# Gates, token projections and pooling input of a two-layer encoder moved to seven block products, with only their seven right operands kept

## Chip, cores and metric

The kernel runs on one core of a Trainium2 chip. The metric is the device time of one execution in microseconds (us); less is better. Engines are named as in the profile: PE is TensorE (matmul), DVE is VectorE, ACT is ScalarE, POOL is GpSimd, SP is SyncE, which issues the loads.

## What is computed

Two layers act on 512 positions of width 1024, all in float32. Cut to what matters:

```
for i in range(2):
    x = LN(a*x + 0.5*swiglu(x, ffn1_up[i], ffn1_down[i]))          # 1024 -> 2*2816 -> 1024
    u,v, q,k,vr,g, pool_in, cq,ckv,kr, gate_logits = split(x @ w_in[i])
    ys = (sgu(u,v), retention(q,k,vr,g), pooling(pool_in), mla(cq,ckv,kr))   # each 256 wide
    merged = sum(sigmoid(gate_logits[:, n]) * (ys[n] @ w_branch[i][n]) for n in range(4))
    x = LN(a*x + merged @ w_out[i])
    ple = sigmoid(x @ w_ple_gate[i]) * (p[i] @ w_ple[i])
    x = LN(a*x + 0.5*swiglu(x, ffn2_up[i], ffn2_down[i]) + ple)
```

w_in has 6304 columns: 512 for sgu (uv), 512 for q and k (qk), 512 for the retention's v and g (vg), 256 for pooling (wp), 416 for latent attention (wm) and 4096 gate columns. The products of x with ffn_up, w_in and w_ple_gate are the "products with the layer's activations" that this document is about.

## The kernel before, in words

**Precision.** Every float32 operand of a large product is kept as a rounded high part and a remainder. `split` (L175) makes them: ACT copies the high part (L177, `whi<-stage`), DVE subtracts it from the source (L178, `wlo<-stage,whi`). `mm3` (L161) then issues three matmuls for each block: low by high, high by low, high by high (L163 to L165).

**Weights.** A weight block of 128x1024 comes by one DMA of 512 KB into a `stage` buffer and is split into a slot, a pair `whi`, `wlo`. There are six slots in a ring and four stage buffers, eight in the feed-forward parts.

**Activations.** After each layer norm the rows are transposed by PE (`lnT`), four 128x128 blocks at a time, and split into `xh`, `xl` (8 x 512 columns). With an index for the half of the features and one for the half of the positions, x consists of B11, B12 (features 0 to 511, positions 0 to 255 and 256 to 511), B21 and B22.

**Seven products.** The feed-forward up-products alone (42 times a unit of 512 output features) are made with seven block products in place of eight (Strassen-Winograd). `up_blocks` (L135) makes the seven left operands from the four weight blocks with four sums on DVE (L138) and seven splits. `unit` (L271) multiplies them with B11, B21, B22 and four combinations T1 to T4 of the B's, kept in `th`, `tl`; each block product is 24 matmuls of 128x256, so 168 a unit. Banks sX, sY and sZ collect them, and three additions on DVE (L289) finish the four result blocks.

**All others are full products.** A gate (`branch`, four branches of eight f's) takes eight weight blocks, 24 matmuls of 128x512, for each f; ACT applies a tanh, six matmuls of 128x512 (`br`) make the branch's output, DVE multiplies and adds. The token projections (`tok_proj`, L580) split four weight blocks and take 24 matmuls of 128x512 for each of the four position blocks: uv, qk, vg, wm (128x416, `mlap`) and the two halves of w_ple_gate (`pg`). The pooling input takes two weight blocks, 24 matmuls each. In layer 1 the first two f's of the first feed-forward part are a full product too (`up`).

**Combinations at the norm.** `norm` (L397) builds T1 to T4 behind the positions 2 and 3 of a norm that precedes a feed-forward part (L428 to L436), not at the norm between the first feed-forward part and the mixers.

**Order.** PE's order is written out by hand: the program text is PE's order, and chains (`norm`, the mixers' small steps) are generators which a weaver (`Weave`) steps when its own clock says that they are ready, or when `need` asks for them. The other engines run their instructions in the order in which the scheduler puts them, each engine in order. In the mixers the order of the program is: uv, sgu, pooling, qk, vg, retention, branch 2, latent attention (`mla`), branches 0, 1, 3, then `w_out` and the norm.

Of the kernel before, what the change touches and what calls it, by code (L numbers as in the profile page):

```python
# [18 lines left out]
P = 128  # L19
# [60 lines left out]
class Trunk:  # L80
# [13 lines left out]

    def __init__(self, tc, ctx, t):
# [8 lines left out]
        self.xh = c.tile([P, KD, SEQ], F32R, tag="xh", name="xh")  # L104
        self.xl = c.tile([P, KD, SEQ], F32R, tag="xl", name="xl")
# [3 lines left out]
        self.tt, self.turn, self.wide = None, False, False  # L109
# [6 lines left out]
    def slot(self):  # L116
        return [self.ring.tile([P, 1024], F32R, tag=q, name=q, bufs=6) for q in ("whi", "wlo")]

    def stage(self):
        self.turn = not self.turn  # L120
        if self.wide and self.turn:
            return self.more.tile([P, 1024], F32, tag="stage", name="stage", bufs=4)
        return self.ring.tile([P, 1024], F32, tag="stage", name="stage", bufs=4)
# [10 lines left out]

    def up_blocks(self, src):  # L135


        add = lambda o, x, y: self.nc.vector.tensor_tensor(o, x, y, op=ALU.add)  # L138

        def get(q):  # L140
            s = self.stage()
            self.load(s, src[:, q, :])
            return s

        a11 = get(0)
        yield self.halves(a11, 1024)
        a21, a22 = get(2), get(3)
        s1 = self.stage()
        add(s1, a21, a22)
        yield self.halves(s1, 1024)  # L150
        add(s1, s1, a11)
        yield self.halves(s1, 1024)
        a12 = get(1)
        yield self.halves(a12, 1024)
        add(a11, a11, a21)
        yield self.halves(a11, 1024)
        add(a12, a12, s1)
        yield self.halves(a12, 1024)
        yield self.halves(a22, 1024)
# [30 lines left out]
    def begin(self, up, fp):  # L190
# [5 lines left out]
        warm = fp.tile([P, SEQ], F32, tag="cc", name="warm", bufs=2)  # L196
        self.nc.vector.memset(warm, 0.0)
        warm = warm.bitcast(F32R)
# [8 lines left out]
        for kk in range(KD // 2):  # L207
# [9 lines left out]
            for j in range(2):  # L217
                self.nc.sync.dma_start(out=x[:, j, :], in_=self.t["xT"][:, 2 * kk + j, :])
                self.split(self.xh[:, 2 * kk + j, :], self.xl[:, 2 * kk + j, :], x[:, j, :])
            for q in range(1, 4):  # L220
                weight(q)
        for kk in range(KD // 2):
            for q, p in enumerate(ps):
                for k in (2 * kk, 2 * kk + 1):
                    self.mm3(p, part([w[0] for w in ws], q, k), part([w[1] for w in ws], q, k),
                             self.xh[:, k, :], self.xl[:, k, :], k == 0, k == KD - 1)
        for j in range(0, HK, 2):
# [4 lines left out]
            for c in range(4):  # L232
                self.split(self.th[:, c, j:j + 2, :], self.tl[:, c, j:j + 2, :], t[c])
# [14 lines left out]
    def open_tt(self):  # L248
        self.tt = ExitStack()
        p = self.tt.enter_context(self.tc.tile_pool(name="tt", bufs=1, reuse_waits="tile"))  # L250
        self.more = p
        self.th, self.tl = [p.tile([P, 4, HK, HT], F32R, tag=q, name=q) for q in ("th", "tl")]

    def close_tt(self):
        self.wide = False
        self.tt.close()

    def open_rows(self):
        self.rows = ExitStack()
        p = self.rows.enter_context(self.tc.tile_pool(name="rows", bufs=1, side="right", reuse_waits="tile"))  # L260
        self.z = [p.tile([P, D], F32, tag=f"z{i}", name=f"z{i}") for i in range(NT)]

    def xop(self, c):

        if c[0] == "T":
            q = int(c[1]) - 1
            return [(self.th[:, q, k, :], self.tl[:, q, k, :]) for k in range(HK)]
        r, s = int(c[1]) - 1, int(c[2]) - 1
        return [tuple(x[:, r * HK + k, s * HT:(s + 1) * HT] for x in (self.xh, self.xl)) for k in range(HK)]

    def unit(self, src, tp):  # L271
# [4 lines left out]
        X, Y, Z = [self.bank(q) for q in ("sX", "sY", "sZ")]  # L276
        cc = tp.tile([P, 2, SEQ], F32, tag="cc", name="cc", bufs=2)
        nb = tp.tile([P, SEQ], F32, tag="nb", name="nb", bufs=2)
        ws = self.up_blocks(src)

        def product(ps, b, first):
            w, x = next(ws), self.xop(b)
            for j in range(2):
                for k, (rh, rl) in enumerate(x):
                    c = slice(j * 512 + k * P, j * 512 + (k + 1) * P)
                    self.mm3(ps[:, j * HT:(j + 1) * HT], w[0][:, c], w[1][:, c], rh, rl,
                             first and j == 0 and k == 0, k == HK - 1, skip_group_check=True)

        add = lambda o, ps: nc.vector.tensor_tensor(o, ps, o, op=ALU.add)  # L289
        product(X, "B11", True)  # L290
        nc.scalar.copy(cc[:, 0], X)
        product(Y, "T1", True)
        nc.scalar.copy(nb, Y)
        product(X, "T2", False)
        nc.scalar.copy(cc[:, 1], X)
        product(Z, "B21", True)
        add(cc[:, 0], Z)
# [99 lines left out]
    def norm(self, z, i, g, b, last, blocks, keep):  # L397
# [15 lines left out]
        for j in range(2):  # L413
# [7 lines left out]
            if not blocks or i < NT // 2:  # L421
                continue
# [679 lines left out]
```

## Time and profile before

| what | value |
|---|---|
| time, median of 3 runs | 2373.01 us (2372.81 to 2373.32) |
| profiled execution, its own time | 2373.37 us |
| its span, first to last instruction | 2371.6 us, so 1.8 us lie around it |
| mean granted TensorE clock | 0.994 of full speed |
| PE busy | 2341.6 us, 99% of the span, 14020 matmuls |
| PE weight loads busy (beside PE) | 2065.3 us, 87% |
| DVE busy | 1572.1 us, 66%, 2230 instructions |
| ACT busy | 908.7 us, 38%, 1200 instructions |
| loads | 246.13 MB, mean 104 GB/s |

The table's shares are means over the whole span. A stage whose engines are loaded in another way is read in the view by windows, which gives each engine's busy time in a stretch. The view of the timeline gives start and duration of single instructions; matmuls overlap, so that the distance of two starts and not the duration tells what one costs.

### The profile page before, as it was taken

What the parts mean: (1) busy time and instruction counts of PE and PEld (TensorE: products, weight loads), DVE (VectorE), ACT (ScalarE), POOL (GpSimd) and SP (SyncE); (2) the same over time, 40 slices, a digit from 0 to 9 for tenths busy, and PEclk for the clock granted to TensorE, in tenths of its full rate; (3) what the DMA queues carried; (4) which work ended last, traced back from release to release, by engine and by line L of the source; (5) the groups of instructions that cost most, each with busy time, mean ns of one, the idle gap of its engine ahead of it and who ended that gap; (6) DMA issues with size and microseconds to landing.
All of it is one profiled execution on the core that took longest, in us unless ns stands there. A gap on an engine that the chain in (4) does not pass through costs nothing.

```text
span 2371.6 us, 33791 instructions
## 1 busy us (share of the span) xinstructions
PE 2341.6 (99%) x14020; PEld 2065.3 (87%) x14020; DVE 1572.1 (66%) x2230; ACT 908.7 (38%) x1200; POOL 55.3 (2%) x93
## 2 busy tenths in 40 slices
PE   9999999999999899999999999999999998999998
PEld 8899897888888698998998998878888886989987
DVE  8777588545445775775896775884454457867757
ACT  6344343234222453443353443442332314534432
POOL 0000001000000000000000000010000000000000
PEclk9999999999999999999999999999999999999999
DMA  6342323222322332423242333232223214323331
GB/s 204 127 125 81 124 98 116 86 82 87 133 98 89 107 106 81 125 82 123 63 135 88 119 104 108 98 122 78 90 80 134 92 60 133 116 80 118 105 107 45
DMA packets 73802, 246.13 MB, mean 104 GB/s; under 512 B 10033, under 2 KB 13233, under 8 KB 73649
## 3 DMA queue, kind: packets, MB, share of 16 engines
q1 hardware_dynamic: 73648, 243.97, 31.9%
q8 instruction: 110, 1.80, 0.3%
q14 instruction: 44, 0.35, 0.0%
HBM read 237.65 MB, written 6.29 MB: 103 GB/s over the span
## 4 chain that ended last, share of the span: by engine, by line
PE 95%; DVE 3%; issue 1%; ACT 1%; DMA 0%; SPq 0%; DVEq 0%; ACTq 0%
PE dn L164 7%; PE dn L165 7%; PE dn L163 7%; PE sX L163 6%; PE sX L165 6%; PE sX L164 6%; PE gate L165 5%; PE gate L163 5%; PE gate L164 5%; PE sY L163 3%; PE sY L165 3%; PE sY L164 3%; PE sZ L164 2%; PE sZ L165 2%; PE sZ L163 2%; PE pg L163 1%
## 5 line engine op out<-in xcount | busy, mean ns | idle before, releaser
L178 DVE TENSOR_TENSOR wlo<-stage,whi 128x1024 fp32r<-128x1024 f32 (+2 forms) x562 | 667.5, 1192 | 431.5 <-ACT whi L177 430.9
L177 ACT CAST whi<-stage 128x1024 fp32r<-128x1024 f32 (+2 forms) x562 | 573.1, 1026 | 615.3 <-PE dn L165 315.8
L163 PE MATMUL sX<-tl,whi 128*128 128x256 f32 x1008 | 282.4, 280 | 0.4 <-DVE nb L289 0.4
L164 PE MATMUL sX<-th,wlo 128*128 128x256 f32 x1008 | 281.4, 279 | 0.4 <-DVE wlo L178 0.3
L165 PE MATMUL sX<-th,whi 128*128 128x256 f32 x1008 | 281.4, 279 | 0.0
L164 PE MATMUL dn<-whi,hp 128*128 128x512 f32 x704 | 278.1, 395 | 1.8 <-DVE hp L178 1.6
L163 PE MATMUL dn<-wlo,hp 128*128 128x512 f32 x704 | 278.8, 396 | 0.0
L165 PE MATMUL dn<-whi,hp 128*128 128x512 f32 x704 | 277.7, 394 | 0.0
L138 DVE TENSOR_TENSOR stage<-stage 128x1024 f32<-128x1024 f32 x168 | 204.7, 1219 | 13.4 <-DMA stage<-up_in 11.9
L163 PE MATMUL gate<-xl,whi 128*128 128x512 f32 x512 | 206.1, 403 | 0.0
L165 PE MATMUL gate<-xh,whi 128*128 128x512 f32 x512 | 202.7, 396 | 0.0
L164 PE MATMUL gate<-xh,wlo 128*128 128x512 f32 x512 | 202.6, 396 | 0.0
L164 PEld LDWEIGHTS sX<-th,wlo 128*128 128x128 f32 x1008 | 189.0, 188 | 0.9 <-DVE wlo L178 0.9
L163 PEld LDWEIGHTS sX<-tl,whi 128*128 128x128 f32 x1008 | 189.2, 188 | 0.6 <-issue 0.6
L165 PEld LDWEIGHTS sX<-th,whi 128*128 128x128 f32 x1008 | 189.5, 188 | 0.0
L164 PEld LDWEIGHTS dn<-whi,hp 128*128 128x128 f32 x704 | 131.9, 187 | 34.3 <-DVE hp L178 3.5
L165 PEld LDWEIGHTS dn<-whi,hp 128*128 128x128 f32 x704 | 131.9, 187 | 32.4
L163 PEld LDWEIGHTS dn<-wlo,hp 128*128 128x128 f32 x704 | 131.9, 187 | 31.1
L632 ACT ACTIVATE gate<-gate 128x512 f32<-128x512 f32 x64 | 38.2, 597 | 228.6 <-PE gate L165 206.3
L165 PEld LDWEIGHTS gate<-xh,whi 128*128 128x128 f32 x512 | 96.3, 188 | 23.0
L164 PEld LDWEIGHTS gate<-xh,wlo 128*128 128x128 f32 x512 | 96.3, 188 | 21.3
L163 PEld LDWEIGHTS gate<-xl,whi 128*128 128x128 f32 x512 | 96.4, 188 | 21.0
(301 smaller groups left out, 4780.6 us busy)
## 6 DMA issues: line engine op xcount, KB each, us to landing
stage<-up_in SPq DMA_DIRECT2D x172, 512.0 KB, 3.9
stage<-dn_in SPq DMA_DIRECT2D x88, 512.0 KB, 3.6
stage<-wg_in SPq DMA_DIRECT2D x64, 512.0 KB, 3.8
stage<-wbr_in SPq DMA_DIRECT2D x16, 512.0 KB, 3.8
stage<-wo_in SPq DMA_DIRECT2D x16, 512.0 KB, 3.6
stage<-wpg_in SPq DMA_DIRECT2D x16, 512.0 KB, 4.0
stage<-wuv_in SPq DMA_DIRECT2D x8, 512.0 KB, 3.5
xs<-z SPq DMA_DIRECT2D x8, 512.0 KB, 2.6
```

The lines of the kernel that those rows point to most:

```text
L138: add = lambda o, x, y: self.nc.vector.tensor_tensor(o, x, y, op=ALU.add)
L163: mm(ps, lh, rl, start=start, stop=False, **more)
L164: mm(ps, ll, rh, start=False, stop=False, **more)
L165: mm(ps, lh, rh, start=False, stop=stop, **more)
L177: self.nc.scalar.copy(hi, src)
L178: self.nc.vector.tensor_tensor(lo, src, hi.bitcast(F32), op=ALU.subtract)
L632: nc.scalar.activation(tg, ps, AF.Tanh, scale=0.5)
```

## The change

1. **One kind of operand.** `xh`, `xl`, `th`, `tl` go; `qh`, `ql` hold seven right operands: B11, B21, B22, T1, T2, T3, T4. B12 is not kept.
2. **All products with the activations are units** (`unit`, L259; `blocks`, L229): a gate unit makes four f's (two units a branch), `tok_unit` (L310) makes uv, qk, vg, the two halves of w_ple_gate and, with 832 columns, wm; wp is a unit of 256 features; the full `up` product in layer 1 becomes a unit. The order of the seven products is B11, B21, then T2, T1, T3, B22, T4.
3. **Early steps.** A unit stops after B11 and B21. Where it is early, this part is issued beside the norm's chain, and weight blocks 0 and 1 are loaded a second time for the sums: uv, qk and vg of each layer, the two halves of w_ple_gate, and the first three up-units of layer 1's first feed-forward part.
4. **Combinations at every norm** but the last, also at that between the first feed-forward part and the mixers.
5. **Space.** Slots: four in the ring, three more in the feed-forward parts only. The rows z stay resident; during the mixers they hold the sums over branches, and the rows come back from scratch behind branch 3. The raw results of the projections are kept in SBUF, and the mixers read them there. Retention's transposes move into its attend chain; the four head chains of `mla` start behind its whole unit, positions 2, 3, 0, 1; branch 2 is followed by a `need` for sgu and retention.

The core of the diff:

```diff
     def slot(self):
-        return [self.ring.tile([P, 1024], F32R, tag=q, name=q, bufs=6) for q in ("whi", "wlo")]
+        self.nslot += 1
+        p, n = (self.more, 3) if self.more and self.nslot % 7 > 3 else (self.ring, 4)
+        return [p.tile([P, 1024], F32R, tag=q, name=q, bufs=n) for q in ("whi", "wlo")]
...
+    def blocks(self, src, n):
...
+        early = (yield) or self.more is None
+        a11 = get(0)
+        yield self.halves(a11, n)
+        a12 = get(1)
+        yield self.halves(a12, n)
+        if early:
+            a11 = get(0)
+        a21, a22 = get(2), get(3)
+        s1 = self.stage()
+        add(s1, a21, a22)
+        add(a21, a21, a11)
+        add(a11, s1, a11)
+        yield self.halves(a11, n)
+        yield self.halves(s1, n)
+        yield self.halves(a21, n)
+        if early:
+            a12 = get(1)
+        add(a12, a12, a11)
+        yield self.halves(a12, n)
+        yield self.halves(a22, n)
...
+        X, Z = bank("sX"), bank("sZ")
+        self.ready(*(range(NT // 2) if not tok else ()))
+        product(X, "B11", True, ws.send(early))
+        nc.scalar.copy(c11, both(X))
+        product(Z, "B21", True, next(ws))
+        v.tensor_tensor(c11, both(Z), c11, op=ALU.add)
+        yield
+        self.ready(*range(NT))
+        Y = bank("sY")
+        product(X, "T2", False, next(ws))
+        nc.scalar.copy(c12, both(X))
+        product(Y, "T1", True, next(ws))
+        nc.scalar.copy(c22, both(Y))
+        product(X, "T3", False, next(ws))
+        v.scalar_tensor_tensor(c22, both(X), -1.0, c22, op0=ALU.mult, op1=ALU.subtract)
+        product(Y, "B22", False, next(ws))
+        v.tensor_tensor(c12, both(Y), c12, op=ALU.add)
+        product(X, "T4", False, next(ws))
+        yield both(X)
...
+            if i < NT // 2:
+                put(j, ps)
+            elif j == 0:
                 self.w.need(self.ln[i - NT // 2])
                 t = self.sums(HK)
...
+            else:
+                put(2, ps)
+                self.combine(t, t[2], part(self.qh, 1).bitcast(F32), ps)
+                nc.vector.tensor_tensor(t[3], t[3], part(self.ql, 1).bitcast(F32), op=ALU.subtract)
+                for c in (1, 2, 3):
+                    put(3 + c, t[c])
...
+            def branch(b, y, first=False, final=None):
+                v = nc.vector
+                for q in range(2):
+                    wb = self.weights(t["wbr"][l, b, q])
...
+                    u = self.unit(t["wg"][l, b, q], 1024, False, G[:, 0:2, a], G[:, 0:2, c], G[:, 2:4, c])
+                    next(u)
...
+                raw = {}
+                for q in ("uv", "qk", "vg"):
+                    raw[q] = cp.tile([P, NT, 512], F32, tag="big8", name=q, bufs=3)
+                us = {q: self.tok_unit(t["w" + q][l], 1024, raw[q], True) for q in raw}
+                for u in us.values():
+                    next(u)
                 y0, y2, y1 = pair(0), pair(2), pair(1)
-                c0 = self.sgu(l, cp, y0)
+                next(us["uv"])
+                c0 = self.sgu(l, cp, y0, raw["uv"])
                 c2 = self.pooling(l, cp, y2)
-                c1 = self.retention(l, cp, y1)
+                next(us["qk"])
+                next(us["vg"])
+                c1 = self.retention(l, cp, y1, raw["qk"], raw["vg"])
                 need(*c2)
-                branch(2, y2)
+                branch(2, y2, True)
                 need(c0)
+                need(c1[0])
+                need(*c1[1])
```

**Where instructions move: DVE, the end of layer 0's norm between the first feed-forward part and the mixers.** z_90 (before) and z_74 (after) are the rows of position block 3. Before:

```order
L406 SCALAR_TENSOR_TENSOR z_90<-z_90,rsln,gb 128x512 x2
L178 TENSOR_TENSOR xl<-lnT,xh 128x4x128
L178 TENSOR_TENSOR wlo<-stage,whi 128x1024 x2
L178 TENSOR_TENSOR xl<-lnT,xh 128x4x128 x2
L923 TENSOR_SCALAR ssq<-ssq 128x512
L924 TENSOR_TENSOR ssq<-ssq,sxh 128x512
```

After:

```order
L420 SCALAR_TENSOR_TENSOR z_74<-z_74,rsln,gb 128x512 x2
L445 TENSOR_TENSOR stage<-ql,lnT 128x512
L446 TENSOR_TENSOR stage<-stage,qh 128x512
L154 TENSOR_TENSOR wlo<-stage,whi 128x1024
L154 TENSOR_TENSOR ql<-stage,qh 128x4x128
L154 TENSOR_TENSOR ql<-lnT,qh 128x4x128
L225 TENSOR_TENSOR stage<-lnT,stage 128x512
L226 SCALAR_TENSOR_TENSOR stage<-stage,lnT 128x512
L295 TENSOR_TENSOR uv<-sZ,uv 128x2x256
L227 SCALAR_TENSOR_TENSOR stage<-stage,qh 128x512
L154 TENSOR_TENSOR ql<-stage,qh 128x4x128
L451 TENSOR_TENSOR stage<-stage,ql 128x512
```

The combinations (L445, L446, L225 to L227, L451, and the splits into ql) now stand between the last norm and the weight splits of the projections, a second such group follows, and the first row of sgu's chain (ssq) stands some 25 rows further on.

**DVE, branch 2 of layer 0, where the gate's weights are split beside the retention's steps.** Before, the first f's:

```order
L859 BN_AGGR gmv<-gst 128x2
L639 SCALAR_TENSOR_TENSOR acc_4255<-gate,br 128x512
L859 BN_AGGR gmv<-gst 128x2
L178 TENSOR_TENSOR wlo<-stage,whi 128x1024
L186 TENSOR_SCALAR rsgn<-gmv 128x4
L861 TENSOR_TENSOR yt<-ro,gmv 128x256
```

After, the first half-branch:

```order
L154 TENSOR_TENSOR wlo<-stage,whi 128x1024 x3
L231 TENSOR_TENSOR stage<-stage 128x1024
L884 TENSOR_TENSOR ke<-qk,dk 128x256
L231 TENSOR_TENSOR stage<-stage 128x1024 x2
L891 TENSOR_TENSOR sd<-rs,dec 128x512
L909 COPY state_4571<-rkv 64x64 x4
L295 TENSOR_TENSOR gate<-sZ,gate 128x2x256
L154 TENSOR_TENSOR wlo<-stage,whi 128x1024 x3
```

One weight split for each f has become a train of seven splits and four sums for four f's, with the additions of the unit (L295) among them.

## Rows read from the trace of the kernel before

**Rows 1.** The page: busy shares, DVE's busy tenths in 40 slices, the load queue.

```profile
PE 2341.6 (99%) x14020; PEld 2065.3 (87%) x14020; DVE 1572.1 (66%) x2230; ACT 908.7 (38%) x1200; POOL 55.3 (2%) x93
...
DVE  8777588545445775775896775884454457867757
...
q1 hardware_dynamic: 73648, 243.97, 31.9%
```

**Rows 2.** The chain that ended last, share of the span by engine.

```profile
PE 95%; DVE 3%; issue 1%; ACT 1%; DMA 0%; SPq 0%; DVEq 0%; ACTq 0%
```

**Rows 3.** Timeline of PE: start and duration in us, then line, operation, tile, shape.

```profile
103.79 0.28 PE L163 MATMUL sX<-xl,whi 128*128 128x256 f32 x1
...
163.21 0.39 PE L163 MATMUL dn<-wlo,hp 128*128 128x512 f32 x1
...
196.81 0.28 PE L163 MATMUL sX<-xl,whi 128*128 128x256 f32 x1
...
507.04 0.35 PE L163 MATMUL mlap<-wlo,xh 128*128 128x416 f32 x1
...
511.92 0.35 PE L165 MATMUL mlap<-whi,xh 128*128 128x416 f32 x1
```

**Rows 4.** DVE's groups by line and shape: busy us, mean ns, idle before.

```profile
L178 DVE TENSOR_TENSOR wlo<-stage,whi 128x1024 fp32r<-128x1024 f32 x534 | 650.2, 1220 | 421.0 <-ACT whi L177 420.3
L138 DVE TENSOR_TENSOR stage<-stage 128x1024 f32<-128x1024 f32 x168 | 204.7, 1219 | 13.4 <-DMA stage<-up_in 11.9
L289 DVE TENSOR_TENSOR cc<-sZ,cc 128x512 f32<-128x512 f32 x42 | 28.8, 685 | 0.7
L178 DVE TENSOR_TENSOR tl<-stage,th 128x512 fp32r<-128x512 f32 x32 | 21.6, 683 | 0.4 <-ACT th L177 0.2
```

**Rows 5.** Timeline of DVE in an up-unit, four instructions back to back.

```profile
121.65 1.21 DVE L138 TENSOR_TENSOR stage<-stage 128x1024 f32<-128x1024 f32 x1
122.78 1.22 DVE L178 TENSOR_TENSOR wlo<-stage,whi 128x1024 fp32r<-128x1024 f32 x1
123.92 0.68 DVE L470 SCALAR_TENSOR_TENSOR cc<-sX,cc 128x512 f32<-128x512 f32 x1
124.52 0.68 DVE L470 SCALAR_TENSOR_TENSOR cc<-nb,cc 128x512 f32<-128x512 f32 x1
```

**Rows 6.** Windows: stretch, its length, busy us of PE, PEld, DVE, ACT, POOL, clock, DMA.

```profile
334.68:507.00 172.32, 172.32 (x818) 140.85 (x817) 111.77 (x238) 53.61 (x87) 15.91 (x28) 1.00 0.29 94
335.00:355.00 20.00, 20.00 (x96) 16.27 (x95) 19.60 (x36) 5.67 (x8) 2.90 (x3) 1.00 0.19 74
...
780.00:800.00 20.00, 12.41 (x49) 10.04 (x50) 16.30 (x24) 10.51 (x15) 0.00 (x0) 0.74 0.32 106
1164.69:1207.16 42.47, 40.81 (x271) 36.92 (x270) 41.81 (x71) 13.66 (x22) 3.69 (x4) 1.00 0.15 45
```

**Rows 7.** Timeline of DVE: the first row addition before the mixers of layer 0.

```profile
334.68 0.69 DVE L511 TENSOR_TENSOR z<-z,dn 128x512 f32<-128x512 f32 x1 [1.52 <-PE dn L165]
```

**Rows 8.** Waits of PE: us in total, times, longest.

```profile
PE pg L163 <- DVE wlo L178: 15.8, 2, 7.9
PE up L163 <- DVE xl L178: 1.7, 1, 1.7
```

**Rows 9.** Timeline of PE at w_ple_gate, layer 0.

```profile
779.27 0.40 PE L165 MATMUL pw<-whi 128*128 128x512 f32 x1
787.59 0.77 PE L163 MATMUL pg<-wlo,xh 128*128 128x512 f32 x1 [7.92 <-DVE wlo L178]
788.15 0.63 PE L164 MATMUL pg<-whi,xl 128*128 128x512 f32 x1
788.58 0.63 PE L165 MATMUL pg<-whi,xh 128*128 128x512 f32 x1
```

**Rows 10.** Timeline of DVE at the norm between the layers: first addition, first weight split behind.

```profile
1164.69 0.69 DVE L511 TENSOR_TENSOR z<-z,dn 128x512 f32<-128x512 f32 x1 [1.53 <-PE dn L165]
...
1207.16 1.22 DVE L178 TENSOR_TENSOR wlo<-stage,whi 128x1024 fp32r<-128x1024 f32 x1
```

More of the change, by code (lines that the diff above doesn't have):

```diff
@@ L116, in slot @@
     def slot(self):
[L117 removed]
+        self.nslot += 1
+        p, n = (self.more, 3) if self.more and self.nslot % 7 > 3 else (self.ring, 4)
+        return [p.tile([P, 1024], F32R, tag=q, name=q, bufs=n) for q in ("whi", "wlo")]
     def stage(self):
[L120 to L123, printed above, removed]
+        self.nstage += 1
+        p = self.more if self.more and self.nstage % 2 else self.ring
+        return p.tile([P, 1024], F32, tag="stage", name="stage", bufs=4)
     def halves(self, src, n):
@@ L263, in xop @@
[L263 to L271, printed above, removed]
-        nc = self.nc
[L276 to L297, printed above, removed]
-        product(X, "T3", False)
-        add(nb, X)
-        product(Y, "B22", False)
-        add(cc[:, 1], Y)
-        product(X, "T4", False)
-        return cc, X, nb
@@ L305, in constants, with tok_unit @@
+    def tok_unit(self, src, n, raw, early=False):
+        w = n // 4
+        u = self.unit(src, n, True, raw[:, 0:2, :w], raw[:, 2:4, :w], raw[:, 2:4, w:], early)
+        next(u)
+        yield
+        self.nc.scalar.activation(raw[:, 0:2, w:], next(u), AF.Copy, scale=-1.0)
+        yield
     def constants(self, scratch):
@@ L395, in stats, with norm @@
         self.nc.vector.bn_stats(self.st[i][:, half, :], z[:, half * 512:(half + 1) * 512])
-    def norm(self, z, i, g, b, last, blocks, keep):
+    def norm(self, z, i, g, b, last, keep):
         nc = self.nc
@@ L537, in ffn_body @@
                 self.load_gb(g, b, l, 1 if which == 1 else 3)
-            while tt < k1:
-                if l == 0 and which == 1 and tt == lead + 2:
+            if first and lead:
+                self.lead(self.begin(up, fp), h, fp)
+                k0 = lead
+            units = []
+            early = first and not lead and which == 1
+            for tt in range(k0, k1, 2):
+                cc = fp.tile([P, 2, SEQ], F32, tag="cc", name="cc", bufs=3)
+                nb = fp.tile([P, SEQ], F32, tag="nb", name="nb", bufs=2)
+                u = self.unit(up[tt // 2], 1024, False, side(cc[:, 0]), side(cc[:, 1]), side(nb), early)
+                units.append((tt, u, cc, nb))
+                if early:
+                    next(u)
+            for tt, u, cc, nb in units:
+                if lead and tt == 2 * lead:
                     self.constants(z[3])
                     self.load_rows(t["x"])
-                self.ready(*range(NT))
-                cc, X, nb = self.unit(up[tt // 2], fp)
-                finish(tt // 2, cc, (X, nb))
-                tt += 2
+                if not early:
+                    next(u)
+                finish(tt // 2, cc, next(u), nb)
+            k0 = CHUNKS[ci][0]
             if tail:
@@ L561, in ple @@
         nc, t = self.nc, self.t
+        raw = [pp.tile([P, NT, 512], F32, tag=f"raw{q}", name="praw") for q in range(2)]
+        pws = [pp.tile([P, NT, 512], F32, tag=f"pws{q}", name="pws") for q in range(2)]
+        us = []
         for half in range(2):
@@ L1073, in layout @@
     o["wo"] = mov(a["w_out"], 512)
-    o["wpg"] = mov(a["w_ple_gate"], 512)
+    o["wpg"] = np.stack([tok(a["w_ple_gate"][:, :, q * 512:(q + 1) * 512]) for q in range(2)], 1)
     o["wple"] = mov(a["w_ple"], 512)[:, 0]
```

355 lines of the change are left out of this document (158 added, 197 removed).

## The prediction

> **What bounds the kernel now.** I read the busy shares first: PE works 99% of the span, DVE 66%, ACT 38%, and the load queue takes 31.9% of its 16 engines [rows 1]. The chain of waits says the same, 95% of what ended last is PE [rows 2]. So what takes matmuls away is worth its full time, as long as the other engines keep up. Whether they do is not read from a mean: DVE's tenths run from 4 to 9 over the span [rows 1]. In the view by windows the reader is to see that in the first 20 us of the norm before layer 0's mixers DVE works 19.60 of 20.00 us while PE still waits for nothing [rows 6]. The new work of DVE falls in just this place. I take 98%, from that row, as what DVE reaches when it is the bound.
>
> **What PE saves.** By PE's instruction lists 2688 matmuls of 128x512 go and 4704 of 128x256 come. Prices by distance of starts [rows 3]: 504 matmuls of 256 columns from 103.79 to 163.21, 0.1179 us each; 144 of 512 columns from 163.21 to 196.81, 0.2333 us each. Saving: 2688 x 0.2333 = 627.1, cost 4704 x 0.1179 = 554.6, so -72.5 us. For wm 192 matmuls of 416 columns go and 336 of 208 come. The old cost (511.92 - 507.04) / 26 = 0.1877 us, together 36.0; the new ones are not in the trace, between half of that (0.0939, 31.5 us in all) and the 256-column price (39.6). I take 0 for the difference, within -4.5 and +3.6.
>
> **What DVE gets.** By the lists 184 more operations of 128x1024 (sums L231 and splits), 14 of 128x832 and about 130 of 512 columns or narrower. A split or sum of 128x1024 has a duration of 1.22 us [rows 4], but back to back it takes 122.78 - 121.65 = 1.13 to 1.14 us, one of 512 columns 124.52 - 123.92 = 0.60 [rows 5]. So about 184 x 1.14 + 14 x 1.0 + 130 x 0.6 = 302 us, 1572 becomes some 1875. Averaged, that still hides: 1875 of 2300 is 82%. ACT gets a copy for each split, some 165 instructions, and stays under half of the span: nothing. The second loads of early units, two of 512 KB for each of 13, add 13.6 MB to 246 where the queue is at a third: nothing, the bound being that a stage buffer comes late, which the DVE term covers since the same buffers wait for DVE's sums.
>
> **The mixers, where it doesn't hide.** Take the stretch from the first row addition (334.68 [rows 7]) to the first matmul of latent attention (507.04 [rows 3]), with uv, wp, qk, vg and branch 2. PE is busy throughout, 172.3 us, DVE 111.8 [rows 6].
> PE afterwards: five units (uv, qk, vg, two half-branches) save 96 x 0.2333 - 168 x 0.1179 = 2.6 us each, wp saves 48 x 0.2333 - 84 x 0.1179 = 1.3: 172.3 - 13.0 - 1.3 = 158.0.
> DVE afterwards: each of the five units has three splits more and four sums, 7 x 1.14 = 8.0, and three additions onto its result, 3 x 0.61 = 1.8 (the row of L289 is the nearest [rows 4]); five times 9.8 is 49.0. wp: seven splits and four sums of 512 columns and three small additions for two splits of 1024, +5.7. The combinations, new at this norm: nine more operations of 512 columns for each of two position blocks, 18 x 0.61 = 11.0 [rows 4]. Sum 111.8 + 49.0 + 5.7 + 11.0 = 177.5 us, at 98% 181.1. So DVE, 60 us under PE before, comes out 23 above it. Behind its last split PE still has 24 x 0.1179 for T4 and 24 x 0.2333 for the branch outputs, 8.4 us. PE waits 181.1 + 8.4 - 158.0 = 31.5 us.
> It isn't given back. DVE is in order: the splits of uv's second part are queued behind the norm's combinations, those of wp and qk behind sgu's chain, and four slots and four stage buffers bar it from running far ahead. In later half-branches DVE needs 8 splits and 4 sums (13.7), 3 additions (1.8) and 8 operations at the outputs (4.9), about 20.4, where PE needs 19.8 + 5.6 = 25.4: there it keeps up, so the loss ends there. Latent attention's head chains behind its whole unit add 2 to 3 us of lag: 34 us a layer, and 2 for the matmuls at a reduced clock behind gaps (rows below), so **+36 a layer, +72**. From below: DVE without any idle, nothing after the last split, 177.5 - 158.0 = 19.5. From above: DVE at 90%, 177.5 / 0.9 + 8.4 - 158.0 = 47.6, with 5 for the clock 53.
>
> **The norm between the layers.** Before, DVE is busy 41.81 of the 42.47 us from the first addition to the first weight split of the next unit [rows 6, 10], and PE waits for xl, 1.7 us [rows 8]. Three early units and T2 need six weight splits, four sums and three additions there, in place of two splits, of two splits of B12 and of one product: 41.8 - 4.1 + 6.8 + 4.6 + 2.3 + 1.8, about 54 us with the split of the next block, at 98% 55. PE has 72 x 0.2333 = 16.8 us of the last down-products, 32 transposes of 128 columns (under 3.8, the price of 256 columns), 144 x 0.1179 = 17.0 of early products and 2.8 of T2, some 41. It waits 14 in place of 1.7, **+12** (from +4, if the splits stand ahead of the combinations, to +14).
>
> **w_ple_gate.** Before, PE waits 7.92 us for wlo, twice, and runs its next matmuls 0.43 to 0.56 us apart in place of 0.2333 [rows 8, 9]; the window has the clock at 0.74 [rows 6]. The early products of one half (5.7 us) fill part of it, but the splits of the second half stand behind the combinations of position 3. I take **+3** each, +6, between 0 and +8 each.
>
> **Sum.** Against the profiled execution's own 2373.37 (span 2371.6, 1.8 around it, 0.4 above the median of the runs): 2373.4 - 72.5 + 72 + 12 + 6 = 2390.9, **2391 us**. The ends of the terms: 2373.4 - 77 + 39 + 4 + 0 = 2339 and 2373.4 - 69 + 106 + 14 + 16 = 2440; the two are not all at one end at once, so I take 2345 to 2437.
>
> **Rivals.**
> *A: DVE's queue hides, PE stays the bound.* Then only the norm between the layers remains: 2373.4 - 72.5 + 12 = 2313. For it: DVE has 34% of the span free [rows 1], and DVE's idle time ahead of the splits, 421 us, ends with ACT's copy [rows 4], so it waits for buffers, not for itself. Against it: the sum over the stretch, 177 to 158. It would decide from the point where DVE did 20 us of the stretch's splits ahead of the first addition. The Trainium skill's page "Perfetto Trace Analysis", section Identifying the Most-Contended Engine, says that the engine with the highest occupancy is the one to relieve first; by that rule the change cuts the right engine and this rival's time would follow. The window of 335 to 355 us disagrees for its stretch, where DVE's 19.60 of 20.00 us leaves nothing free.
> *B: half hidden.* DVE is ahead by half of the waits, because weight splits at the start were done during the last down-products: 2373.4 - 72.5 + 36 + 12 + 6 = 2355. This is the rival on the faster side with the most weight.
> *C: the engines wait for each other in turn.* PE's order issues the early steps of three units ahead of uv's rest; PE holds slots until a late product, DVE then waits for slots, and DVE's busy share stays at 90%: +53 a layer, and each gap costs clock, as in the window 780 to 800 us, 0.74 [rows 6]: 2373.4 - 72.5 + 106 + 14 + 16, near 2437 and beyond. For it: four slots in place of six. Against it: an early unit holds a slot only during its product.
> *D: no columns are saved.* If matmuls of 256 columns cost clearly more than half of those of 512, the saving goes: break-even at 627.1 / 4704 = 0.1333 us; then 2373.4 + 72 + 12 + 6 = 2463. The rows say 0.1179 against 0.1167, 1% more. The same page, section Matmuls, says that larger matmuls are more efficient than smaller ones; here rows 3 agree only to that 1%, which is in the sum.
>
> **Chances.** Forecast with DVE's order as the bound, 0.58; A 0.10; B 0.17; C 0.12; D 0.03. The range leaves out A, D and about half of C. A measurement of this kernel can tell about 0.2%, 4.7 us. Faster by more than that, below 2368: A, B, together 0.27. Within it: the low edge of the forecast, 0.10. Slower, above 2378: 0.63.
>
> **What would show it.** Right, if PE's busy time falls by about 70 us while its idle time grows to some 90, if the waits name DVE's wlo and ql ahead of sX and sY, if DVE in the stretch before latent attention is above 93% busy, and if the later branches show no waits. DVE's share should be near 79%. Wrong, if PE's waits at the mixers are under 10 us a layer (A), if DVE there is far below 90% while PE waits for it, by slots or a late ACT copy or load (C), or if matmuls of 256 columns start more than 0.125 us apart (D).

## The result, and the profile after

The changed kernel takes **2648.86 us** (median of 4 runs, 2647.18 to 2654.03) against 2373.16 (2372.81 to 2373.73): ratio 1.1165, 95% interval 1.1146 to 1.1184. The forecast was 2391, range 2345 to 2437; the sign was right, the size was not: 276 us more where 18 were forecast. Its profiled execution has a span of 2648.3 us, 276.7 over that of before. Busy shares and the clock in 40 slices, from the page of the changed kernel (to be read against [rows 1] and the table of before):

```profile
PE 2380.5 (90%) x16180; PEld 2212.6 (84%) x16180; DVE 1897.4 (72%) x2574; ACT 1059.7 (40%) x1393; POOL 58.2 (2%) x101
...
PEclk9999987998999789999979999978999997899999
```

DVE's work grew about as counted (1897 us, forecast 1875). PE should have been busy 72.5 us less and is busy 38.9 us more, and it is idle for 268 us in place of 30. The idle time is gaps; of the 111 us that PE is busier than it should be, 88 are slow steps of matmuls, as shown below. The waits of PE, changed kernel (us in total, times, longest; before: [rows 8]):

```profile
PE sX L139 <- DVE wlo L154: 88.8, 13, 11.5
PE sX L140 <- DVE wlo L154: 48.9, 22, 6.6
PE sX L139 <- ACT whi L153: 39.5, 17, 5.0
PE sZ L139 <- DVE wlo L154: 29.6, 6, 5.1
PE pw L139 <- DVE wlo L154: 18.8, 4, 7.1
```

The gaps have places. In both traces the starts of the last down-products, of `w_out` and of the first down-products cut the span into parts; the feed-forward parts between them kept their length within 0.3 us, the last one within 0.8. By windows, first before, then after (stretch, length, busy us of PE, PEld, DVE, ACT, POOL, clock, DMA):

```profile
329.50:726.60 397.10, 396.55 (x1895) 327.30 (x1894) 223.75 (x468) 131.71 (x229) 19.81 (x36) 1.00 0.30 99
726.60:900.20 173.60, 165.68 (x970) 145.08 (x969) 127.81 (x158) 69.08 (x84) 3.96 (x4) 0.97 0.32 105
1159.50:1251.10 91.60, 89.06 (x659) 83.79 (x658) 84.61 (x114) 40.64 (x53) 3.69 (x4) 1.00 0.32 104
```

```profile
329.40:809.40 480.00, 404.43 (x2794) 378.55 (x2794) 353.87 (x613) 190.69 (x304) 21.37 (x40) 0.91 0.34 108
809.40:1023.00 213.60, 174.16 (x1113) 159.89 (x1113) 152.96 (x184) 85.45 (x104) 3.96 (x4) 0.89 0.32 107
1282.20:1410.10 127.90, 99.77 (x634) 92.38 (x633) 98.11 (x124) 46.63 (x58) 3.69 (x4) 0.85 0.32 107
365.00:395.00 30.00, 12.36 (x72) 11.77 (x70) 16.89 (x25) 10.31 (x15) 0.00 (x0) 0.78 0.32 94
```

The mixers of layer 0 (norm included) grew by 82.9 us, the part from `w_out` through w_ple_gate by 40.0, the norm between the layers by 36.3; layer 1's mixers by 81.2 and its second part by 37.4: together 277.8. DVE is *not* busy in the longer stretches: 353.87 of 480 us, 74%, and in the 30 us from 365 on 16.89, with PE at 12.36. Neither engine is full there; they work in turn. One such turn, beside the norm of layer 0, on PE, ACT and DVE (start, duration, line, operation, and in brackets the idle time ahead with what ended it):

```profile
356.70 0.60 PE L149 MATMUL lnT<-ident,z 128*128 128x128 f32 x4
361.91 0.58 PE L139 MATMUL sZ<-wlo,qh 128*128 128x256 f32 x1 [4.62 <-DVE wlo L154]
...
364.64 1.06 PE L149 MATMUL lnT<-ident,z 128*128 128x128 f32 x4
...
365.70 0.41 PE L140 MATMUL sZ<-whi,ql 128*128 128x256 f32 x1
365.92 0.41 PE L141 MATMUL sZ<-whi,qh 128*128 128x256 f32 x1
...
367.22 0.28 PE L141 MATMUL sZ<-whi,qh 128*128 128x256 f32 x1
373.64 0.55 PE L139 MATMUL sX<-wlo,qh 128*128 128x256 f32 x1 [6.15 <-DVE wlo L154]
373.99 0.41 PE L140 MATMUL sX<-whi,ql 128*128 128x256 f32 x1
```

```profile
365.73 0.59 ACT L153 CAST qh<-lnT 128x512 fp32r<-128x512 f32 x1 [4.36 <-PE lnT L149]
...
371.20 1.04 ACT L153 CAST whi<-stage 128x1024 fp32r<-128x1024 f32 x1
```

```profile
360.64 1.22 DVE L154 TENSOR_TENSOR wlo<-stage,whi 128x1024 fp32r<-128x1024 f32 x1
...
366.35 0.69 DVE L154 TENSOR_TENSOR ql<-lnT,qh 128x512 fp32r<-128x512 f32 x1 [3.89 <-ACT qh L153]
...
372.27 1.23 DVE L154 TENSOR_TENSOR wlo<-stage,whi 128x1024 fp32r<-128x1024 f32 x1 [0.26 <-ACT whi L153]
```

PE's second transposes of position block 2 (364.64) stand behind half of uv's B21 product, which waits for its split (wlo, 360.64). ACT and then DVE wait for these transposes (4.36 and 3.89 us), DVE makes the combinations, only then comes the next weight block's split (372.27), and PE starts qk's B11 after 6.15 us. The same goes on for qk and vg. Behind the gap of 4.62 us the granted clock was 0.50, the lower of the two levels (1.2 in place of 2.4 GHz), as this window shows:

```profile
361.91:366.13 4.22, 4.22 (x19) 4.22 (x20) 0.55 (x1) 0.40 (x1) 0.64 (x1) 0.50 0.58 137
```

PE steps there by 365.92 - 365.70 = 0.22 us, where a step at the full clock takes 0.118; the first step behind a gap is longer still (373.99 - 373.64 = 0.35). Counted over the trace, 831 steps of 256 columns in the units take 0.19 to 0.70 us (6 before). What they take above 0.118 sums to 88 us, 73 of it in 777 steps of 0.19 to 0.26 us.

### The profile page after: what moved, and what is told of

The parts are those of the page before. It is cut to its first block, busy times and chain, and to the rows that moved or that the text cites. A ratio compares the mean times of both kernels' runs of the same rounds, so it can differ in the third digit from the quotient of the medians.

```text
span 2648.3 us, 38826 instructions
## 1 busy us (share of the span) xinstructions
PE 2380.5 (90%) x16180; PEld 2212.6 (84%) x16180; DVE 1897.4 (72%) x2574; ACT 1059.7 (40%) x1393; POOL 58.2 (2%) x101
## 2 busy tenths in 40 slices
DMA packets 83905, 279.62 MB, mean 106 GB/s; under 512 B 11153, under 2 KB 14353, under 8 KB 83729
## 5 line engine op out<-in xcount | busy, mean ns | idle before, releaser
L154 DVE TENSOR_TENSOR wlo<-stage,whi 128x1024 fp32r<-128x1024 f32 (+3 forms) x659 | 774.3, 1185 | 400.4 <-ACT whi L153 399.9
L153 ACT CAST whi<-stage 128x1024 fp32r<-128x1024 f32 (+3 forms) x659 | 661.8, 1019 | 714.3 <-PE dn L141 305.3
L140 PE MATMUL sX<-qh,wlo 128*128 128x256 f32 x1920 | 556.1, 290 | 48.9 <-DVE wlo L154 48.9
L139 PE MATMUL sX<-ql,whi 128*128 128x256 f32 x1920 | 557.4, 290 | 39.5 <-ACT whi L153 39.5
L141 PE MATMUL sX<-qh,whi 128*128 128x256 f32 x1920 | 552.8, 288 | 0.0
L140 PEld LDWEIGHTS sX<-qh,wlo 128*128 128x128 f32 x1920 | 376.2, 196 | 54.8 <-DVE wlo L154 53.9
L231 DVE TENSOR_TENSOR stage<-stage 128x1024 f32<-128x1024 f32 (+2 forms) x292 | 351.0, 1202 | 98.2 <-DMA stage<-wg_in 31.5
L139 PEld LDWEIGHTS sX<-ql,whi 128*128 128x128 f32 x1920 | 375.2, 195 | 44.2 <-ACT whi L153 43.2
L141 PEld LDWEIGHTS sX<-qh,whi 128*128 128x128 f32 x1920 | 376.1, 196 | 0.0
L139 PE MATMUL dn<-wlo,hp 128*128 128x512 f32 x704 | 277.8, 395 | 0.0
L141 PE MATMUL dn<-whi,hp 128*128 128x512 f32 x704 | 276.7, 393 | 0.0
L139 PE MATMUL sY<-ql,whi 128*128 128x256 f32 x960 | 273.2, 285 | 0.0
## 6 DMA issues: line engine op xcount, KB each, us to landing
stage<-up_in SPq DMA_DIRECT2D x178, 512.0 KB, 3.6
stage<-wg_in SPq DMA_DIRECT2D x96, 512.0 KB, 4.1
stage<-dn_in SPq DMA_DIRECT2D x88, 512.0 KB, 3.3
stage<-wpg_in SPq DMA_DIRECT2D x24, 512.0 KB, 4.5
stage<-wbr_in SPq DMA_DIRECT2D x16, 512.0 KB, 4.6
stage<-wo_in SPq DMA_DIRECT2D x16, 512.0 KB, 3.5
stage<-wuv_in SPq DMA_DIRECT2D x12, 512.0 KB, 4.0
stage<-wqk_in SPq DMA_DIRECT2D x12, 512.0 KB, 4.0
```

Source lines behind the costliest of these rows:

```text
L139: mm(ps, lh, rl, start=start, stop=False, **more)
L140: mm(ps, ll, rh, start=False, stop=False, **more)
L141: mm(ps, lh, rh, start=False, stop=stop, **more)
L153: self.nc.scalar.copy(hi, src)
L154: self.nc.vector.tensor_tensor(lo, src, hi.bitcast(F32), op=ALU.subtract)
L231: add = lambda o, x, y: self.nc.vector.tensor_tensor(o[:, :n], x[:, :n], y[:, :n], op=ALU.add)
```

## The experiments

Sixteen kernels were run, one execution each beside one of the kernel before (2372.2 to 2374.7 in all). The four runs of the changed kernel lie 6.9 us apart, so a difference of a few us between single runs says nothing. Times in us; the parts are those of layer 0's mixers, of `w_out` to the down-products in layer 0, and of the norm between the layers.

| kernel | time | mixers | w_out part | between layers |
|---|---|---|---|---|
| before | 2373 | 397.1 | 173.6 | 91.6 |
| after | 2649 | 480.0 | 213.6 | 127.9 |
| slots6 | 2634.3 | 474.1 | 210.4 | 123.7 |
| stage8 | 2547.7 | 450.0 | 188.4 | 121.4 |
| noearly | 2589.2 | 459.9 | 204.4 | 121.4 |
| ahead | 2593.9 | 465.2 | 207.3 | 113.1 |
| own | 2553.6 | 451.3 | 194.2 | 128.9 |
| s8ahead | 2509.9 | 444.6 | 184.2 | 111.3 |
| nosum | 2510.7 | 427.0 | 196.4 | 125.3 |
| noT | 2571.9 | 442.8 | 212.9 | 128.1 |
| own_look | 2540.8 | 451.7 | 194.0 | 112.7 |
| late_comb | 2534.6 | 452.4 | 190.5 | 114.2 |
| late_look | 2531.7 | 449.7 | 190.9 | 113.6 |
| gates_only | 2443.1 | 419.3 | 177.2 | 106.6 |
| own_nosum | 2413.0 | 403.4 | 180.1 | 109.4 |
| fill | 2835.8 | 512.0 | 246.0 | 182.3 |
| s8own | 2467.8 | 426.9 | 175.4 | 110.5 |
| s8own_nosum | 2397.4 | 401.8 | 172.3 | 103.0 |

**Slots or stage buffers?** In both, T1 and T2 share a tile, and T3 and T4.

```diff
-        p, n = (self.more, 3) if self.more and self.nslot % 7 > 3 else (self.ring, 4)
+        p, n = (self.more, 1) if self.more and self.nslot % 7 > 5 else (self.ring, 6)
```

> Six slots in the ring outside the feed-forward parts in place of four (seven in all inside them, as before). To have the room, T1 and T2 share one storage and T3 and T4 another, so products with T1 and T3 read the wrong operand; amounts of work and their order stay. Buffer theory (four slots keep the splits from running ahead): the mixers fall from 480 us to under 430, the time under 2520. Lockstep theory (early steps, norm chain and splits stand in one another's queues): little, 2600 to 2645. Amount theory (DVE has too much work): nothing, over 2635.

15 us, with the shared tiles in it: the two slots that the change took away are not the loss.

```diff
-        p = self.more if self.more and self.nstage % 2 else self.ring
-        return p.tile([P, 1024], F32, tag="stage", name="stage", bufs=4)
+        return self.ring.tile([P, 1024], F32, tag="stage", name="stage", bufs=8)
```

> Eight stage buffers everywhere in place of four outside the feed-forward parts; room as in the run with six slots (T1 and T2, T3 and T4 share storage, so those products read the wrong operand). Buffer theory in the form that loads come late: the waits of the sums for their loads (DVE stage from DMA, 31 us for the gates alone) go, time under 2580. Lockstep theory: 2600 to 2645. Amount theory: over 2635.

101 us: of the buffers, the stage ring is the one. In the last gates its waits are gone: from 640 us to `w_out`, PE is busy 145.14 of 145.80 us with eight stage buffers (first row), 157.50 of 169.40 in the changed kernel (second row, 14 matmuls more), where DVE's last sum of a unit waits for the second load of a weight block (third row, DVE's timeline there).

```profile
640.00:785.80 145.80, 145.14 (x1084) 136.41 (x1084) 115.46 (x152) 69.39 (x96) 0.00 (x0) 1.00 0.44 144
```

```profile
640.00:809.40 169.40, 157.50 (x1098) 146.38 (x1097) 123.55 (x161) 69.11 (x98) 0.00 (x0) 0.95 0.38 123
```

```profile
760.26 1.23 DVE L231 TENSOR_TENSOR stage<-stage 128x1024 f32<-128x1024 f32 x1 [3.19 <-DMA stage<-wg_in]
```

**Early steps, and the order of the splits.** `noearly` issues each unit in one piece; `ahead` asks for B21's split before B11's product.

```diff
-                for u in us.values():
-                    next(u)
...
-        product(X, "B11", True, ws.send(early))
+        w1, w2 = ws.send(early), next(ws)
+        product(X, "B11", True, w1)
```

> No early steps anywhere: every unit issues B11 and B21 directly ahead of its other five products; the combinations at the norms and the four slots stay. Lockstep theory: the gaps beside the norms shrink, the stretch from w_out to the down-products from 213.6 to under 195 us, the one between the layers from 127.9 to under 110, the mixers by 20 or more: 2530 to 2590. Amount theory: PE has less to fill the norm with, 2650 to 2690. Buffer theory: within 15 us of 2649.

> In every unit the weight split for B21 is asked for ahead of the product with B11 and not behind it; nothing else. Lockstep theory: the waits ahead of sZ beside the norms (4.9 and 5.4 us in each mixer part, 5.4 at w_ple_gate, 4.0 and 4.1 between the layers) go, time 2590 to 2625. Amount theory: within 10 us of 2649. Buffer theory: 2640 to 2665, since the slots are taken earlier.

60 and 55 us less. Both totals lie at the edge of the lockstep's ranges, `noearly` at the small end (2589.2, with less at the two later parts than expected, 204.4 and 121.4 us), `ahead` at the large end (2593.9). With four stage buffers, steps that were begun early to fill the norm made the parts beside it longer.

**Combinations out of the ring.** `own` takes the norm's sums from the gate buffer (or a tile of the w_ple_gate part's pool); operands and results are those of the changed kernel.

```diff
+        if self.comb and nk == HK:
+            t = self.comb().rearrange("p q (k n) -> p q k n", k=HK)
+            return [t[:, q] for q in range(4)]
         a, b = [self.stage().rearrange(
```

> The norm's combinations get a buffer of their own at the norms ahead of the mixers and ahead of w_ple_gate (the gate buffer, free there, or one in that part's pool) and take none of the four stage buffers. Stage theory, form 1 (the gain of the run with eight stage buffers, 101 us, came from the combinations that hold two of four): 2550 to 2590, with the stretch behind w_out near 190 us. Form 2 (it came from the units' own six loads and a sum, which four buffers can't hold): 2635 to 2650. Amount theory: over 2635.

95 us, the first form; the mixers give 29 and 30 of it, the parts behind `w_out` 19 and 20. The ring is handed out in program order, so that a weight load which follows a combination in it waits until that combination has been made, and this waits for PE. SyncE's rows show it. In the changed kernel the second block of uv and all of qk and vg are issued behind the first rows of the norm, and between 364 and 395 us SyncE waits three times for the split of a combination (ql):

```profile
353.05 0.37 SPq L157 DMA_DIRECT2D stage<-wuv_in  x1
...
366.73 4.91 SPq L157 DMA_DIRECT2D stage<-wqk_in  x2
373.52 10.32 SPq L157 DMA_DIRECT2D stage<-wvg_in  x2
```

```profile
SPq L157 <- DVE ql L154: 13.4, 3, 8.9
```

In `own` all six early blocks are issued by 333.1 us, ahead of the norm's row stores:

```profile
304.77 2.75 SPq L157 DMA_DIRECT2D stage<-wuv_in  x2
318.49 6.51 SPq L157 DMA_DIRECT2D stage<-wqk_in  x2
329.89 3.20 SPq L157 DMA_DIRECT2D stage<-wvg_in  x2
```

SyncE's own order has a part in this that no run took out by itself: uv's second block is issued right behind a row store that had waited for the norm (352.63), qk's first block behind the constants of sgu and pooling, without a wait of its own. With own buffers four weight splits stand among the rows of the norm (DVE's timeline of `own`; compare 372.27 above). The windows from 350 to 390 us, `own` and then the changed kernel, have DVE at 36.94 and 24.55 of 40 us:

```profile
356.65 1.22 DVE L154 TENSOR_TENSOR wlo<-stage,whi 128x1024 fp32r<-128x1024 f32 x1
...
358.39 1.22 DVE L154 TENSOR_TENSOR wlo<-stage,whi 128x1024 fp32r<-128x1024 f32 x1
...
359.63 1.18 DVE L154 TENSOR_TENSOR wlo<-stage,whi 128x1024 fp32r<-128x1024 f32 x1
...
364.03 1.22 DVE L154 TENSOR_TENSOR wlo<-stage,whi 128x1024 fp32r<-128x1024 f32 x1
```

```profile
350.00:390.00 40.00, 27.86 (x209) 26.78 (x208) 36.94 (x55) 16.75 (x24) 4.17 (x8) 0.87 0.33 102
```

```profile
350.00:390.00 40.00, 22.74 (x134) 21.24 (x132) 24.55 (x38) 11.21 (x18) 3.61 (x8) 0.79 0.37 114
```

`noT` leaves the combinations at the mixers' norm out (`elif keep: ... put(2, ps)`).

> The combinations T1 to T4 are left out at the norm between the first feed-forward part and the mixers of each layer (products there read those of an earlier norm): 18 fewer operations of 512 columns on DVE, and none of the stage buffers taken. Amount theory: 11 us of DVE a layer, 2625 to 2630. Lockstep theory (splits and transposes wait behind the combinations in turn): 20 to 40 us a layer, 2570 to 2610.

77 us for 27 us of DVE's work (1897.4 to 1870.4 busy): what the combinations cost is what they hold up. The products with T1 to T4 have nothing to wait for here either, so that this run does not tell buffers from order; `own` does.

**Both, and what adds.** `s8ahead` joins stage8 and ahead, `s8own` stage8, own and ahead.

> Eight stage buffers everywhere and the split for B21 asked for ahead of the product with B11 (T1 and T2, T3 and T4 share storage as in the run with eight stage buffers, so those products read the wrong operand). If loads that come late and splits that stand behind the norm's chain are two separate losses, the gains of 101 and 55 add: 2490 to 2500. If they are one loss seen twice: 2530 to 2550. Amount theory: over 2520 in any case, with DVE over 90% busy where PE waits.

> Eight stage buffers, combinations in their own buffer, B21's split ahead of B11's product (T1 and T2, T3 and T4 share storage, so products with T1 and T3 read the wrong operand). Two losses (combinations hold stage buffers beside the norms; the units' own loads and sums find none in the gates): 2440 to 2480, with the mixers near 430 us. One loss seen twice: 2500 to 2515, as the run with eight stage buffers and the earlier split.

`s8ahead` came out between its two cases, `s8own` in the range of two losses: 181 us less than the changed kernel.

**Program order alone.** With own and ahead: `own_look` asks for the later splits two products ahead, `late_comb` puts `yield 14.0` between `put(2, ps)` and `combine`, `late_look` does both.

> Combinations in their own buffer, B21's split asked for ahead of B11's product, and in each unit's second part every split asked for two products ahead of its use (T2 and T1 together, then one more ahead of each product). Queue-order theory (a split stands behind copies and additions that wait for PE): the gaps of 1.3 and 4.2 us behind sZ in the gates go, the stretch from the mixers to w_out falls by 20 from 450, time 2460 to 2500. Amount theory: as the run with own buffers alone less the 15 us a part that the earlier B21 split gave, 2500 to 2530.

> Combinations in their own buffer, B21's split ahead of B11's product, and T2 to T4 built in the program 14 us behind B22's split, so that the early units' splits stand ahead of them on DVE. Queue-order theory: the gap before uv's T2 (12.4 us with own buffers) falls under 8, the norm between the layers under 110 us: 2470 to 2510. Amount theory: DVE has the same work ahead of T2, nothing gained against own buffers and the earlier split, 2500 to 2530.

> Both: the late combinations and the splits two products ahead. Queue-order theory: the gains add, 2440 to 2480, still over 2373 because sgu's, pooling's and retention's steps, the norm and seven splits and four sums a unit are one queue on DVE. If it falls under 2373, the amount of DVE's work was no obstacle at all and the forecast's mechanism is wrong, not only its size.

13, 19 and 22 us less than `own`, which is about what `ahead` gives at the norm between the layers (128.9 to some 113 in all three); the mixers stay at 450. All three missed every range that was set for them. They say that with the combinations out of the ring these orders move nothing in the mixers. They do not say that order has no weight: `noearly` and `ahead` change nothing else and gave 60 and 55 us.

**The amount of DVE's work.** `nosum`, `own_nosum` and `s8own_nosum` take the 292 sums (315 us of DVE, 1897.4 to 1582.9) out of the changed kernel, of own with ahead, and of `s8own`.

```diff
-        s1 = self.stage()
-        add(s1, a21, a22)
-        add(a21, a21, a11)
-        add(a11, s1, a11)
         yield self.halves(a11, n)
-        yield self.halves(s1, n)
+        yield self.halves(a22, n)
```

> No sums of weight blocks (292 operations, 351 us of DVE): the products with T2, T1, T3 and T4 use single weight blocks, so the product is not the reference's; loads, splits and matmuls stay in number, and one stage buffer a unit is no longer taken. Amount theory (DVE has too much work, as forecast): the mixers fall to under 400 us, time 2330 to 2430. Lockstep and stage theories: the places beside the norms keep most of their gaps, since no sum stands there, the later gates lose theirs; 2480 to 2560.

> Combinations in their own buffer, B21's split ahead of B11's product, and no sums of weight blocks (products with T2, T1, T3, T4 use single blocks, so the result is not the reference's; 351 us of DVE's work gone, 66% becomes its share of before). Amount theory: what is left over 2310 goes, 2330 to 2400. Lockstep and queue theory: the chains of split after split on ACT and DVE with four slots still stand, 2430 to 2490.

> The kernel with eight stage buffers, own buffers for the combinations and the earlier B21 split, without the sums of weight blocks (products with T2, T1, T3, T4 use single blocks; T1 and T2, T3 and T4 share storage). Amount theory, the forecast's mechanism at its own size: 60 to 110 us less than 2468, 2360 to 2410. If what is left are chains (norm, sgu, latent attention's heads, one queue for each engine) and not the amount: 2420 to 2468.

138, some 128 (against `own_look`) and 70 us. The amount theory's range for `nosum` was missed: the changed kernel is 137 us over before even with DVE's work at its old size. `own_nosum`, 2413.0, lies between its two cases. With four stage buffers a unit without sums also needs one buffer less, so the third run, where buffers are least short, is the cleanest: the amount of sums costs 70 us, inside the 60 to 110 of the forecast's mechanism. By parts it is 25 and 27 in the two layers' mixers, 3 and 1 behind `w_out`, 8 between the layers, and 7 ahead of the first mixers, in a part that the change did not touch. Windows over the mixers of layer 0, `s8own` and `s8own_nosum`:

```profile
336.50:763.40 426.90, 384.93 (x2794) 361.38 (x2793) 348.34 (x613) 190.82 (x304) 21.72 (x40) 0.96 0.37 118
```

```profile
329.55:731.40 401.85, 378.57 (x2795) 356.11 (x2794) 296.63 (x561) 191.19 (x304) 21.38 (x40) 0.98 0.40 126
```

**Only the gates.** `gates_only` makes all but the gates and latent attention's projection from eight block products with four splits, no sums, nothing early.

```diff
+        if full:
+            ws = [self.weights(src[:, q, :], n) for q in range(4)]
...
+            for ps, q in ((X, 0), (Z, 2)):
+                product(ps, "B11", True, ws[q])
+                product(ps, "B21", False, ws[q + 1])
```

> Only the gates and latent attention's projection stay seven-product units: uv, qk, vg, wp, the halves of w_ple_gate and layer 1's first up-unit are made from eight block products of 128x256 with four splits and no sums, and no step is early. T1 stands for B12, which is not kept, and T1 to T4 share one storage, so those products read wrong operands; the room gives six slots and six stage buffers; combinations in their own buffer. If the losses belong to units next to a norm: the part behind w_out and that between the layers return to 174 to 180 and 92 to 96 us, the mixers fall to 375 to 400, time 2335 to 2385. If the gates lose by themselves (queue of DVE in every half-branch): the mixers stay above 420, time over 2420. PE without any wait would give 2373 less 2 x 21 = 2331.

Neither case: 2443.1. The part behind `w_out` returned to 177.2 us, but `s8own` brings it to 175.4 with its units kept, so that it is not the units as such that cost there. The part between the layers came to 106.6, not to 92 to 96. The mixers stayed at 419.3, with gaps of 4.5 and 6.6 us beside the norm and of 3.0 and 5.3 us at latent attention. In the last gates no gap is over 1.4 us.

**The clock.** `fill` puts matmuls of the identity ahead of the early products.

```diff
+            for _ in range(48):
+                nc.tensor.matmul(ps[:, :P], self.ident, self.ident, start=True, stop=True)
```

> The changed kernel with 48 matmuls of 128x128 of the identity into a spare bank (about 4.2 us) ahead of B11, of B21 and of T2 in each early unit; nothing else. Clock theory (of the 275 us about 90 are matmuls at the lower clock behind gaps): PE's clock rises from 0.942 to over 0.96, and the time falls by 20 to 60, since the fill stands in gaps of 4 to 12 us. Rival, the gaps cost only their own length: 13 units by 3 by 4.2 us, the part of it that doesn't fit a gap is added, 2650 to 2760.

Mis-sized: each of these counts as two records, 3744 in all, and PE is busy 352 us more, 9.0 and not 4.2 us for each of the 39 fills. 187 us came on top of 2649; the other 165 stood in gaps, and the clock rose to 0.982. The slow steps fell from 831 to 365, which agrees with a clock that falls in gaps, but the run does not give its price. Both ranges were missed.

## Why the prediction was wrong

**PE's saving: right.** Steps of 256 columns outside gaps are 0.118 us apart, and the feed-forward parts are unchanged. With the buffers mended and the sums out (`s8own_nosum`), PE is busy 2299.9 us, 41.7 under before; of the 30.8 that are missing to 72.5, slow steps hold 25. Rival D is out.

**DVE's amount: near in size, wrong as the only cause.** The forecast gave PE's wait as DVE's sum over PE's sum, at DVE's 98% from the norm of before [rows 6]: 36 us for each layer's mixers, 90 in all parts. In that row DVE hardly waited. In the stretch from the first row addition to the first matmul of latent attention DVE's work came out as forecast, 180.07 us for 177.5 (third figure of busy time below). But the stretch took 233.38 us, where the forecast has 158.0 + 31.5 = 189.5, and DVE was busy 77% of it, not over 93%.

```profile
334.25:567.63 233.38, 178.64 (x1214) 168.87 (x1213) 180.07 (x320) 82.98 (x128) 17.39 (x32) 0.87 0.32 100
```

Where the buffers are mended, the sums cost 70 us, and `own` shows the forecast's picture beside the norm: DVE at 92% from 350 to 390 us while PE waits up to 12.2 (waits of PE in `own`: us in total, times, longest):

```profile
PE sX L139 <- DVE wlo L154: 58.9, 6, 12.2
```

**The step that failed** is the sentence that costs a stage buffer that comes late at nothing, because "the DVE term covers" it. It is a term of its own, and the largest. Eight stage buffers alone give 101 us, own buffers for the combinations alone 95, and both with the earlier split 181 (2649 to 2468). Of the 348 us between 2649 and the 2301 that PE's saving alone would give, these are 181, the sums 70, and 96 are open. What was missed is who shares the ring: the norm's combinations hold two of its four buffers and wait for PE's transposes, these stand behind early products, and those wait for weight splits whose loads come behind the combinations in the same ring. The forecast saw that four buffers keep DVE from running ahead; it did not follow the circle. That is rival C's mechanism, engines that wait in turn, given 0.12 and priced at 53 us a layer where the mixers lost 113 (82.9 longer and the 30 saved). C also named slots, and `slots6` says it was not these.

**The count of loads** was off too: `early = (yield) or self.more is None` holds for every unit outside the feed-forward parts, early or not, so that all of these load two blocks twice. That makes 66 second loads, 58 of them of 512 KB, and not 26; the loads grew from 246.13 to 279.62 MB. DVE's sums wait for such loads (the row at 760.26 us); no run took the second loads out by themselves.

**w_ple_gate and the norm between the layers** were forecast at +3 and +12; less what their units save, they lost about 44 (twice) and 39. For w_ple_gate it was the same failed step: with the buffers mended its part is at 175.4 us, near the forecast's 171. Between the layers it was not: there the units had eight stage buffers from the start, and `own` changes nothing (128.9). The earlier split for B21 brings that part to 113.1, and `s8own` to 110.5, where the forecast gives 101: what was missed there is a wait by order, a split that stands behind the norm's chain.

**The clock** was priced at 2 us a layer, from one stretch at 0.74 [rows 6]. The slow steps cost 88 us, behind 33 gaps of 3 us and more where there had been 2. The Trainium skill's page "TensorE: Matmul & The Clock Gate", section "HAM oscillation — how this bites in real kernels", says that a wait for an operand's load brings the clock down and that the next tile then starts at the lower level; the trace agrees for a wait for a split (4.62 us idle, then a granted clock of 0.50).

**Rivals A and B.** A rested on whole-span shares. PE is still the busiest engine after (90%, and its weight loads 84%, against DVE's 72%), so the rule of the Trainium skill's page "Perfetto Trace Analysis", section Identifying the Most-Contended Engine, that the prediction cites with A, would name the same engine while the kernel lost 276 us. The next section of that page of the Trainium skill, Optimization Strategy, has the sentence that fits: the same gap, repeated on the engine that should be full, can mean that there is no room for the next tile. `stage8` and `own` agree, with 101 and 95 us. B needed weight splits that were done during the last down-products; the second block of uv was loaded only at 353.05 us, at their end.

**Still open:** 2397.4 is 96 us over the 2301 that PE's saving alone would give, some 35 of it in each layer's mixers. Gaps before w_ple_gate's `pw` (9.6 us, twice; before the change 7.9 before `pg`), between the layers (6.0), at sgu and pooling, at latent attention's head chains (up to 2.8) and at the norms are seen in that trace; none was taken out by itself. No variant beats the kernel before; `late_look`, the fastest that leaves nothing out, is 117 us faster than the changed kernel and 159 slower than before.

## What to carry to other kernels

When work is moved next to a dependent chain, draw the circle through all queues and shared buffers before summing any engine's work: a ring that is handed out in program order ties every user to the slowest one ahead of it, and a sum of busy times can't show that. The sign here was DVE at 56 to 77% in stretches in which PE waited for it; a buffer of its own for the slow user was the cheapest remedy. Price gaps on PE with what follows them: here 73 us of matmuls at the lower clock came on top of the idle time.

## What the runs showed that was not expected

A buffer that was idle at that time (the gate's, 4 x 512 numbers of 4 bytes in each partition), with a like pair beside w_ple_gate, was worth 95 us, nearly as much as four more stage buffers outside the feed-forward parts (101). Taking 315 us of work from DVE was worth 138 us with four stage buffers and 70 with eight: part of what looks like an engine's load is the room that its operations hold. The filler on PE was no cheap way to hold the clock: 352 us of it covered 165 us of gaps and added 187.
